# All moving operands of the large matmuls at one place relative to the weights, and new rates for VectorE

## The chip, the cores and the metric

The kernel runs on one core of a Trainium2 chip. The core has TensorE (PE in the profile; its weight loads are listed apart as PEld), VectorE (DVE), ScalarE (ACT), GpSimd (POOL) and SyncE (SP, which here issues the DMAs). The metric is the device time in microseconds of one execution, median over runs.

## The reference

One inference step of a two-layer backbone for two groups of requests that share all weights: 128 context tokens (`x_prompt`) and 128 latent tokens (`x_sample`), model width 2048. Cut to its shape:

```python
for l in range(2):
    mod = silu(cond) @ w_ada[l] + b_ada[l]            # 2048 -> 6 x 2048
    sh1, sc1, gt1, sh2, sc2, gt2 = split(mod, 6)
    h = rmsnorm(x, g_norm_mix[l]) * (1 + sc1) + sh1
    m = mixer_ab(h, ...) if l % 2 == 0 else mixer_c(h, ...)
    x = x + gt1 * m
    h = rmsnorm(x, g_norm_ffn[l]) * (1 + sc2) + sh2
    u = conv3(h @ w_up[l]) + b_conv                   # 2048 -> 2 x 5632, width-3 conv over tokens
    x = x + gt2 * ((silu(u_gate) * u_val) @ w_down[l])
return rmsnorm(x, g_final), new context tensors
```

`mixer_ab` is latent attention and grouped-query attention side by side (one input projection `w_in_ab`, two up-projections `w_q_up` and `w_kv_up`, one output projection `w_out_ab`); `mixer_c` is differential attention (`w_in_c`, `w_out_c`). Everything is float32. The latent tokens attend to 128 cached context keys as well, and the context group also returns its keys and values.

## The kernel before, in words

Features lie on the 128 partitions and tokens along the row, so one tile of activations is 128 features by 256 tokens (both groups side by side, `NT = 256`). All large products go through one function, `gemm` (lines 234 to 244): for each block of 128 x 128 weights it issues three matmuls of 256 columns, `wh*xh`, `wh*xl` and `wl*xh`, where the weights and the activations are split into a rounded part (`wh`, `xh`) and a rest (`wl`, `xl`), so that the product is nearly that of float32. Each matmul has a weight load of its own.

The weights stream in. `Weights.chunk` (line 209) lets SP load 1 MB into a `raw` buffer (three of them), ScalarE rounds it to `wh` (line 195), VectorE subtracts to get `wl` (line 196); `wh` and `wl` have four buffers of eight blocks each, every block 512 bytes of a partition's row.

The moving operands are rows of `ROW = 2 * NT + 8` floats, that is 520 floats or 2080 bytes: 256 of `xh`, 256 of `xl`, eight unused. Such rows make up `hx` (16 rows, the modulated input of a stage, and also the output of the first mixer's heads), `o_all` (16 rows, output of the odd layer's heads) and the `g` tiles (22 tiles, the gated FFN activations). Two smaller operands have other shapes: `ql` (rows of 2048 bytes, for `w_q_up`) and `kv_in` (rows of 384 floats, for `w_kv_up`).

The stages, in order: `w_in_ab` in four parts (its input chunks are ready one quarter after another); heads; `w_out_ab`; FFN of layer 0 as two halves, each `up` (44 groups of 16 blocks) and `down` (16 groups of 22 blocks); `w_in_c` with the odd layer's heads; `w_out_c`; FFN of layer 1; the last norm. Between stages `modulated` (line 445) makes the next `hx`: the sum of squares is finished on PE (`stat_rstd`, lines 175 and 176), `rv` (166), a power on POOL (168), `diag` (182), `spread` on PE (190), then for each of 16 chunks a product `nt` (430), scale and shift (436 on VectorE, 439 on ScalarE), rounding (440) and the rest (442, VectorE or POOL in turn). `fill` (line 401) puts row units there for PE.

The products `silu(cond) @ w_ada`, nearly 200 loads of 1 MB, are spread over the whole time in two ways. `row_step` (line 339) loads a tile `araw` (two buffers) and sums it on PE with four matmuls a tile (`sum_rows`, line 334). `feature_step` (line 311) does one half of a tile on VectorE: a product of 2048 elements with a row sum (line 319, its output tile is called `junk`); two steps share one load into `araw`, eight steps make one unit of `FEATS`, and the steps are kept in program order.

`pump` (line 384) is called after each `gemm` and adds a rate to what is due; a `feature_step` runs whenever a whole one is due. In the FFN the rates are `FRATE` (line 51): one for each `up` group (none for the first six groups of a layer) and one for each `down` group (none for the last four of half 1). At the end of `ffn` a loop runs what is left up to the stage's limit (`FLIMIT`, 13 units, or 104 steps, for layer 0; 15 units in all for layer 1). A scheduler then orders each engine's instructions by its own estimate of time.

Of the kernel before, what the change touches and what calls it, by code (L numbers as in the profile page):

```python
# [17 lines left out]
P = 128  # L18
# [1 line left out]
KD = D // P  # L20
T = 128
NT = 2 * T
ROW = 2 * NT + 8
NL = 2
GRID_W = 64
EPS = 1e-6
# [21 lines left out]
    _n += _w  # L48
NCONST = _n
RATE = {"in": 0.4, "in3": 0.25, "heads": 0.85, "out0": 1.2, "c": 0.65, "outc": 0.65}  # L50
FRATE = {"up": 0.75, "down": 1.55}
PEW = {"heads": 1.0, "out0": 1.0, "c": 0.5}
QUIET = [4, 3, 3]
LATE = 3
# [21 lines left out]
def step_kernel(ctx: ExitStack, tc: tile.TileContext, A: dict):  # L76
# [4 lines left out]
    wpool = ctx.enter_context(tc.tile_pool(name="wpool", bufs=3))  # L81
# [8 lines left out]
    def banks(name):  # L90
        return tc.tile_pool(name=name, bufs=1, space=PSUM)
# [3 lines left out]
    def nm(s):  # L95
        uid[0] += 1
        return f"{s}_{uid[0]}"

    def T_(pl, shape, tag, dt=F32, bufs=None):
        kw = {} if bufs is None else {"bufs": bufs}  # L100
        return pl.tile(shape, dt, tag=tag, name=nm(tag), **kw)


    cst = T_(keep, [P, NCONST], "cst")
# [21 lines left out]
    def load_cw(l):  # L126
        ada["cw"] = T_(keep, [P, 4, 2 * NFF], "convw")
        sp.dma_start(out=ada["cw"], in_=A["wconv"][:, l])
# [65 lines left out]
    def split(out_hi, out_lo, src):  # L194
        act.copy(out_hi, src)  # L195
        dve.tensor_tensor(out=out_lo, in0=src, in1=out_hi.bitcast(F32), op=ALU.subtract)  # L196
# [37 lines left out]
    def gemm(blocks, xh, xl, n=NT, first=0):  # L234

        ps = T_(pacc, [P, 512], "acc")
        last = len(blocks) - 1
        for i in range(last + 1):
            k = (i + first) % (last + 1)
            wh, wl = blocks[k]  # L240
            pe.matmul(ps[:, :n], wh, xh(k), start=(i == 0), stop=False)  # L241
            pe.matmul(ps[:, :n], wh, xl(k), start=False, stop=False)  # L242
            pe.matmul(ps[:, :n], wl, xh(k), start=False, stop=(i == last))  # L243
        return ps[:, :n]
# [60 lines left out]
    def load_row():  # L305
        feat["row"] = T_(feat["home"], [P, 2, D], "condb")
        sp.dma_start(out=feat["row"], in_=A["condb"])
        for r in range(2):
            act.activation(feat["row"][:, r], feat["row"][:, r], AF.Silu)
# [74 lines left out]
    def pump(rows, feats=0.0, until=None):  # L384

        until = until or RLIMIT[stage[0]]
        step()
        ada["due"] += rows
        while ada["due"] >= 0.25:
            if ada["i"] >= until and not later:  # L390
                ada["due"] = 0.0
                break
            dve_or_none = ada["i"] >= until or ada["i"] in SUMMED
            ada["due"] -= 0.25 if dve_or_none else 0.25 * ada["pew"]
            row_step(until)
        feat["due"] += feats
        while feat["due"] >= 1.0 and feat["i"] < FLIMIT[stage[0]]:
            feat["due"] -= 1.0
            feature_step()
# [13 lines left out]
    def ensure(l, j, qs=range(4)):  # L413
        for u in [(l, j, q) for q in qs]:
            while u in ROWS and ada["i"] <= ROWS.index(u):
                row_step()
            while u in FEATS and u not in done:
                feature_step()
            while u not in done:
                later.pop(0)()  # L420


    def norm_scale(st):
        return spread(diagonal(stat_rstd(st, D), (0, 1)))

    def modulate(hx, rb, l, which, chunks):

        for c in chunks:
            h = T_(tmp, [P, NT], "nt", bufs=4)
            dve.tensor_tensor(out=h, in0=x[:, c], in1=rb, op=ALU.mult)  # L430
            for g in range(2):
                s = slice(g * T, (g + 1) * T)
                a_ = scl[:, l, which, c, g:g + 1]
                b_ = mod[:, l, 3 * which, c, g:g + 1]
                if g == 0:
                    dve.tensor_scalar(out=h[:, s], in0=h[:, s], scalar1=a_, scalar2=b_,  # L436
                                      op0=ALU.mult, op1=ALU.add)
                else:
                    act.activation(h[:, s], h[:, s], AF.Identity, scale=a_, bias=b_)
            act.copy(hx[:, c, :NT], h)  # L440
            eng = pool if c % 2 else dve
            eng.tensor_tensor(out=hx[:, c, NT:2 * NT], in0=h, in1=hx[:, c, :NT].bitcast(F32),
                              op=ALU.subtract)

    def modulated(st, l, which, units):
        ensure(l, 3 * which + 1)
        ensure(l, 3 * which)
        hx = T_(keep, [P, KD, ROW], "hx", F32R)
        modulate(hx, norm_scale(st), l, which, range(KD))
# [75 lines left out]
    def mixer_ab(hx, rb0, st):  # L525
        l = 0
        with tc.tile_pool(name="ab", bufs=1) as ab:
            with tc.tile_pool(name="abp", bufs=1) as pj:
                kv_in = T_(ab, [P, 4, 2, 3 * T], "kv_in", F32R)
                ckc = T_(pj, [P, 4, T], "ckc")  # L530
                kr = T_(ab, [P, 3 * T], "kr")
# [125 lines left out]
            with tc.tile_pool(name="abh", bufs=1) as hp:  # L657
                ada["pew"] = PEW["heads"]

                o = T_(keep, [P, KD, ROW], "hx", F32R)  # L660
                load_cw(0)
# [79 lines left out]
    def mixer_c(cp, hx, st):  # L741
# [12 lines left out]
        W = Weights(A["w_in_c"], KD, 1)  # L754
        xh, xl = (lambda k: hx[:, k, :NT]), (lambda k: hx[:, k, NT:2 * NT])
        outs = []
        o_all = T_(cp, [P, KD, ROW], "oall", F32R)

        def project(h):
# [98 lines left out]
    def ffn(hx, l, st):  # L858
        xh, xl = (lambda k: hx[:, k, :NT]), (lambda k: hx[:, k, NT:2 * NT])
        W = Weights(A["w_up"][l], KD, 1)  # L860
        WD = Weights(A["w_down"][l], KQ, TB)
        cw = ada["cw"]
        with tc.tile_pool(name=f"ffn{l}", bufs=1) as fp, banks(f"pffn{l}") as pf:
            feat["home"], feat["pool"] = fp, pf

            def conv(ps, m):
                y = T_(fp, [P, NT], "cv", bufs=3)
                act.activation(y, ps, AF.Identity, scale=cw[:, 1, m:m + 1], bias=cw[:, 3, m:m + 1])  # L868
                y3 = y.rearrange("p (g t) -> p g t", g=2)
                p3 = ps.rearrange("p (g t) -> p g t", g=2)  # L870
                dve.scalar_tensor_tensor(out=y3[:, :, 1:], in0=p3[:, :, :T - 1],  # L871
                                         scalar=cw[:, 0, m:m + 1], in1=y3[:, :, 1:],
                                         op0=ALU.mult, op1=ALU.add)
                dve.scalar_tensor_tensor(out=y3[:, :, :T - 1], in0=p3[:, :, 1:],  # L874
                                         scalar=cw[:, 2, m:m + 1], in1=y3[:, :, :T - 1],
                                         op0=ALU.mult, op1=ALU.add)
                return y

            def up(q):
                gs = []  # L880
                for i in range(q * KQ, (q + 1) * KQ):
                    rate = 0 if i < LATE else FRATE["up"]
                    fine[0] = False
                    gate = conv(gemm(W.chunk(), xh, xl), i)
                    pump(0, rate)
                    if i == 0:
                        load_row()
                    val = conv(gemm(W.chunk(), xh, xl), NFF + i)
                    pump(0, rate)
                    act.activation(gate, gate, AF.Silu)  # L890
                    dve.tensor_tensor(out=val, in0=gate, in1=val, op=ALU.mult)
                    g = T_(fp, [P, ROW], "g", F32R, bufs=KQ)
                    split(g[:, :NT], g[:, NT:2 * NT], val)
                    gs.append(g)
                return gs

            def down(gs, q):
                for c in range(KD):
                    quiet = q == NQ - 1 and c >= KD - QUIET[0]
                    fine[0] = quiet  # L900
                    ps = gemm(WD.chunk(), lambda k: gs[k][:, :NT], lambda k: gs[k][:, NT:2 * NT])
                    residual(ps, l, 1, c, st if q == NQ - 1 else None)
                    pump(0, 0 if quiet else FRATE["down"])

            for q in range(NQ):
                gs = up(q)
                if q == 0:
                    ensure(l, 5)
                down(gs, q)
            while feat["i"] < FLIMIT[stage[0]]:  # L910
                feature_step()


    with banks("pab") as ppool["ada"]:
# [6 lines left out]
        for c in range(KD):  # L921
            stat_add(st, x[:, c], KD)
        hx = T_(keep, [P, KD, ROW], "hx", F32R)
        rb0 = norm_scale(st)
# [7 lines left out]
    with tc.tile_pool(name="cc", bufs=1) as cp, banks("pc") as ppool["ada"]:  # L932
        ada["pool"] = cp
        ppool["att"] = ppool["ada"]
        hx = modulated(st, 1, 0, 2)
        load_cw(1)
        st = stat_init()
        ada["pew"] = PEW["c"]
        mixer_c(cp, hx, st)
        hx = modulated(st, 1, 1, 2)  # L940
# [136 lines left out]
```

## Time and profile before

| | |
|---|---|
| median of three runs | 2475.45 us (2472.75 to 2478.08) |
| the profiled execution | 2474.37 us, span 2472.3 us |
| TensorE busy | 2408.7 us, 97% of the span |
| VectorE busy | 1766.5 us, 71% |
| ScalarE busy | 1156.3 us, 47% |
| bytes moved by DMA | 612.92 MB, mean 248 GB/s |

How to read it: times are microseconds from the first instruction unless marked ns. A group of instructions is a line with its engine, operation, `out<-in` by the kernel's names, shapes and count, then busy time and mean ns of one, then the engine's idle time before it and what ended most of that. Matmuls are pipelined, so the length of one says little; the distance between starts is what it costs. A row of busy time by stretch has the stretch, its length, and for each engine the busy time and the count of instructions that touch it, then PEclk (the TensorE clock that was granted, 1.00 is full), the DMA engines' busy share and GB/s; its last row sums all stretches. In a row in order of time stand the start, the length, the engine (a q behind it marks its queue, which issues DMAs), the line, the operation, and in square brackets the idle time before it and what ended it.

### The profile page before, as it was taken

The page shows a single profiled execution, that of the slowest core. Times are in us where ns is not written, and L with a number is a line of the kernel's source. Part 1 is how long each engine was busy: PE and PEld are TensorE (multiplying, and loading weights), DVE is VectorE, ACT ScalarE, POOL GpSimd, SP SyncE. Part 2 cuts the span into 40 slices and gives each one's busy share as a digit, 9 for nine tenths or more (in the row PEclk, how much of TensorE's full clock was granted, in tenths as well). Part 3 has the DMA queues.
Part 4 walks back from the last instruction along what each step waited for, and adds up shares of the span by engine and source line. Part 5 has one row for each costly group of instructions (what it writes and reads, how often), then busy time and mean ns, then how long its engine had stood idle before and what let it go on. Part 6 is the DMA issues. An engine that isn't in the chain of part 4 may idle for free.

```text
span 2472.3 us, 47301 instructions
## 1 busy us (share of the span) xinstructions
PE 2408.7 (97%) x19664; PEld 2268.5 (92%) x19664; DVE 1766.5 (71%) x2699; ACT 1156.3 (47%) x1815; POOL 170.4 (7%) x211
## 2 busy tenths in 40 slices
PE   6999999999999999999999999999999999999997
PEld 4778768799999999999979999897999999999997
DVE  2457534578898999999869897766897655666654
ACT  4335544454553345554455454446545433555442
POOL 2002101100000000001210101021000000000011
PEclk9999999999999999999999999999999999999999
DMA  9886668867677776677776777757665555555553
GB/s 383 311 322 244 231 259 305 320 252 251 255 265 272 292 269 252 250 267 273 279 281 241 275 255 269 279 205 283 242 243 188 188 188 188 186 184 184 183 188 117
DMA packets 92549, 612.92 MB, mean 248 GB/s; under 512 B 9968, under 2 KB 17840, under 8 KB 20400
## 3 DMA queue, kind: packets, MB, share of 16 engines
q1 hardware_dynamic: 92336, 609.91, 67.5%
q8 instruction: 154, 2.52, 0.4%
q14 instruction: 59, 0.48, 0.1%
HBM read 605.12 MB, written 4.75 MB: 247 GB/s over the span
## 4 chain that ended last, share of the span: by engine, by line
PE 94%; DMA 2%; issue 1%; DVE 1%; ACT 1%; POOL 0%; POOLq 0%; SPq 0%; DVEq 0%; ACTq 0%
PE acc L241 29%; PE acc L242 29%; PE acc L243 29%; PE ada L334 4%; DMA araw<-w_ada 1%; PE att L505 1%; DMA ckc<-cache_ckv 1%; PE ada L282 1%; DMA raw<-w_in_ab 0%; PE att L795 0%; DMA raw<-w_ada 0%; PE att L495 0%; DVE x L946 0%; PE ada L269 0%; DVE nt L436 0%
## 5 line engine op out<-in xcount | busy, mean ns | idle before, releaser
L195 ACT CAST wh<-raw 128x1024 fp32r<-128x1024 f32 (+1 forms) x788 | 792.0, 1010 | 1097.2 <-PE acc L242 937.7
L196 DVE TENSOR_TENSOR wl<-raw,wh 128x1024 fp32r<-128x1024 f32 (+1 forms) x788 | 923.8, 1181 | 457.1 <-ACT wh L195 454.3
L241 PE MATMUL acc<-hx,wh 128*128 128x256 f32 x4208 | 1192.7, 285 | 10.9 <-ACT hx L440 10.1
L242 PE MATMUL acc<-hx,wh 128*128 128x256 f32 x4208 | 1186.1, 282 | 0.0
L243 PE MATMUL acc<-hx,wl 128*128 128x256 f32 x4208 | 1185.3, 282 | 0.0
L241 PEld LDWEIGHTS acc<-hx,wh 128*128 128x128 f32 x4208 | 794.0, 189 | 47.8 <-ACT hx L440 19.7
L242 PEld LDWEIGHTS acc<-hx,wh 128*128 128x128 f32 x4208 | 797.2, 190 | 20.5 <-issue 18.7
L243 PEld LDWEIGHTS acc<-hx,wl 128*128 128x128 f32 x4208 | 796.6, 189 | 12.2 <-issue 12.1
L243 PE MATMUL acc<-g,wl 128*128 128x256 f32 x1408 | 394.4, 281 | 0.0
L241 PE MATMUL acc<-g,wh 128*128 128x256 f32 x1408 | 393.9, 280 | 0.0
L242 PE MATMUL acc<-g,wh 128*128 128x256 f32 x1408 | 393.6, 280 | 0.0
L319 DVE CUSTOM_DVE_ANT_0 junk<-araw,condb 128x2048 f32<-128x2048 f32 x120 | 275.4, 2295 | 0.0
L242 PEld LDWEIGHTS acc<-g,wh 128*128 128x128 f32 x1408 | 265.3, 188 | 0.0
L243 PEld LDWEIGHTS acc<-g,wl 128*128 128x128 f32 x1408 | 265.1, 188 | 0.0
L241 PEld LDWEIGHTS acc<-g,wh 128*128 128x128 f32 x1408 | 264.7, 188 | 0.0
L161 POOL TENSOR_TENSOR sqacc<-sqacc,sq 128x256 f32<-128x256 f32 x76 | 91.3, 1201 | 1595.9 <-issue 1274.1
L334 PE MATMUL ada<-araw,condw 128*32 128x512 f32 x864 | 123.3, 646 | 18.8 <-DMA araw<-w_ada 17.9
L363 DVE SCALAR_TENSOR_TENSOR aacc<-araw,condw,aacc 128x512 f32<-128x512 f32 x150 | 107.8, 749 | 0.3
L456 DVE SCALAR_TENSOR_TENSOR x<-acc,mod,x 128x128 f32<-128x128 f32 x192 | 58.3, 345 | 59.6 <-PE acc L243 59.5
L868 ACT ACTIVATE cv<-acc,convw 128x256 f32<-128x256 f32 x176 | 98.4, 559 | 0.0
L874 DVE SCALAR_TENSOR_TENSOR cv<-acc,convw,cv 128x254 f32<-128x254 f32 x176 | 84.3, 479 | 3.7
L871 DVE SCALAR_TENSOR_TENSOR cv<-acc,convw,cv 128x254 f32<-128x254 f32 x176 | 83.8, 476 | 0.0
(195 smaller groups left out, 1625.5 us busy)
## 6 DMA issues: line engine op xcount, KB each, us to landing
araw<-w_ada SPq DMA_DIRECT2D x188, 1024.0 KB, 6.1
raw<-w_up SPq DMA_DIRECT2D x176, 1024.0 KB, 4.8
raw<-w_down SPq DMA_DIRECT2D x88, 1024.0 KB, 4.8
raw<-w_in_c SPq DMA_DIRECT2D x48, 1024.0 KB, 5.2
raw<-w_in_ab SPq DMA_DIRECT2D x20, 1024.0 KB, 7.2
raw<-w_out_ab SPq DMA_DIRECT2D x16, 1024.0 KB, 6.8
raw<-w_out_c SPq DMA_DIRECT2D x16, 1024.0 KB, 4.8
raw<-w_q_up SPq DMA_DIRECT2D x6, 768.0 KB, 4.5
```

The costliest lines, as they stand in the source:

```text
L161: pool.tensor_tensor(out=st["acc"], in0=st["acc"], in1=sq, op=ALU.add)
L195: act.copy(out_hi, src)
L196: dve.tensor_tensor(out=out_lo, in0=src, in1=out_hi.bitcast(F32), op=ALU.subtract)
L241: pe.matmul(ps[:, :n], wh, xh(k), start=(i == 0), stop=False)
L242: pe.matmul(ps[:, :n], wh, xl(k), start=False, stop=False)
L243: pe.matmul(ps[:, :n], wl, xh(k), start=False, stop=(i == last))
L319: tc.keep_in_program_order(dve.tensor_tensor_reduce(out=T_(feat["pool"], [P, D], "junk"), in1=feat["row"][:, c], in0=feat["raw"].rearrange ...
L334: i = pe.matmul(ada["ps"][32 * g:32 * g + 32, :], condw[:, 4 * t + g, :], raw[:, g], start=(t == 0), stop=(t == 3), skip_group_check=True)
L363: i = dve.scalar_tensor_tensor(out=acc[:, c], in0=raw[:, g], scalar=condw[:, k, c:c + 1], in1=acc[:, c], op0=ALU.mult, op1=ALU.add)
L868: act.activation(y, ps, AF.Identity, scale=cw[:, 1, m:m + 1], bias=cw[:, 3, m:m + 1])
L871: dve.scalar_tensor_tensor(out=y3[:, :, 1:], in0=p3[:, :, :T - 1], scalar=cw[:, 0, m:m + 1], in1=y3[:, :, 1:], op0=ALU.mult, op1=ALU.add)
L874: dve.scalar_tensor_tensor(out=y3[:, :, :T - 1], in0=p3[:, :, 1:], scalar=cw[:, 2, m:m + 1], in1=y3[:, :, :T - 1], op0=ALU.mult, op1=ALU.add)
```

## The change

`ROW` loses its eight unused floats, so each row is 2048 bytes, a multiple of 512. Since a weight block is 512 bytes, a moving operand's address relative to the weights, modulo 512, is then the same for every block of a tensor. Unused tiles (`pad`) are put ahead of `kv_in`, `o_all` and the FFN's tiles, and one of 192 bytes into the weights' pool, so that this place is 448 bytes for all of `hx`, `ql`, `kv_in`, `o_all` and `g`. Before, `ql` and `kv_in` were at place 0 and the others moved on by 32 bytes from row to row through all sixteen places. The two rates in `FRATE` are lowered.

```diff
-ROW = 2 * NT + 8
+ROW = 2 * NT
+SHIFT = 448
...
-FRATE = {"up": 0.75, "down": 1.55}
+FRATE = {"up": 0.735, "down": 1.435}
...
+    T_(wpool, [P, 48], "pad", bufs=1)
...
             with tc.tile_pool(name="abp", bufs=1) as pj:
+                T_(ab, [P, SHIFT // 4], "pad")
                 kv_in = T_(ab, [P, 4, 2, 3 * T], "kv_in", F32R)
...
+        T_(cp, [P, SHIFT // 4 - 24], "pad")
         o_all = T_(cp, [P, KD, ROW], "oall", F32R)
...
         with tc.tile_pool(name=f"ffn{l}", bufs=1) as fp, banks(f"pffn{l}") as pf:
             feat["home"], feat["pool"] = fp, pf
+            T_(fp, [P, SHIFT // 4], "pad")
```

## The prediction

> **What bounds the kernel now.** I read the page first (busy time, clock, chain of waits), then busy time by stage, then the matmuls by the place of their moving operand, and last the gap before the odd layer in order of time.
>
> ```profile
> span 2472.3 us, 47301 instructions
> PE 2408.7 (97%) x19664; PEld 2268.5 (92%) x19664; DVE 1766.5 (71%) x2699; ACT 1156.3 (47%) x1815; POOL 170.4 (7%) x211
> ...
> PE 94%; DMA 2%; issue 1%; DVE 1%; ACT 1%; POOL 0%; POOLq 0%; SPq 0%; DVEq 0%; ACTq 0%
> ...
> L241 PE MATMUL acc<-hx,wh 128*128 128x256 f32 x4208 | 1192.7, 285 | 10.9 <-ACT hx L440 10.1
> ...
> L241 PE MATMUL acc<-g,wh 128*128 128x256 f32 x1408 | 393.9, 280 | 0.0
> ...
> L319 DVE CUSTOM_DVE_ANT_0 junk<-araw,condb 128x2048 f32<-128x2048 f32 x120 | 275.4, 2295 | 0.0
> ```
>
> TensorE is the chain (94%). The three lines of `gemm` (241 to 243) have 3 x 4208 matmuls from `hx` and `o`, and 3 x 1408 from `g`; a mean of 285 ns is the length of one in the pipeline, not its price. The price is the time from one start to the next, which whole stages without a gap give:
>
> ```profile
> core 0: us, PE busy (x) PEld busy (x) DVE busy (x) ACT busy (x) POOL busy (x), PEclk, DMA share, GB/s
> 745.80:870.05 124.25, 124.25 (x1059) 124.25 (x1058) 114.48 (x133) 47.28 (x48) 0.00 (x0) 1.00 0.76 284
> 870.05:1119.90 249.85, 249.85 (x2114) 249.85 (x2113) 227.86 (x291) 125.52 (x174) 0.00 (x0) 1.00 0.71 259
> 2083.30:2333.20 249.90, 249.90 (x2115) 249.90 (x2114) 162.08 (x218) 125.74 (x174) 0.00 (x0) 1.00 0.53 186
> ```
>
> The first is a down half (16 x 22 x 3 = 1056 matmuls; the count has two or three more that reach in): 124.25 / 1056 = 117.7 ns. The others are up halves (44 x 16 x 3 = 2112): 118.3 ns. Both at full clock and with PE never idle. VectorE's busy share there, 91% and 92% in layer 0 but 65% in layer 1, does not show in the price. So the bound is what one matmul with its weight load costs.
>
> **Does the place matter?** In the kernel before, a row of `hx` or `g` is 2080 bytes = 4 x 512 + 32, and a weight block 512 bytes, so the moving operand's place relative to the weights moves by 32 bytes from block to block: upwards in the stages that read `hx`, `o` and `o_all` (in `up` it begins at 128), downwards in `down`, where the `g` buffers are met in falling order. `ql` has rows of 2048 bytes and stands at place 0 throughout. I cut the trace at the start of each block's first matmul and summed stretches of equal place modulo 256 (places 256 apart measured alike).
>
> ```profile
> sum 30.57, PE 30.57; mean PE 0.35
> sum 31.38, PE 31.38; mean PE 0.36
> sum 31.63, PE 31.63; mean PE 0.36
> sum 10.21, PE 10.21; mean PE 0.12
> sum 10.56, PE 10.56; mean PE 0.12
> sum 45.11, PE 45.11; mean PE 0.35
> sum 68.05, PE 68.05; mean PE 0.35
> sum 67.22, PE 67.22; mean PE 0.35
> sum 15.04, PE 15.04; mean PE 0.12
> sum 22.62, PE 22.62; mean PE 0.12
> ...
> 223.41:225.44 2.03, 2.03 (x19) 1.00 0.84 315
> ...
> sum 21.27, PE 21.27; mean PE 2.36
> ```
>
> Rows 1 to 3: the 88 blocks (264 matmuls) of the up half at 2083.30 at places 192 (which is 448 too), 0 and 32: 115.8, 118.9 and 119.8 ns a matmul; 192 is the lowest of the eight places, 32 the highest. Rows 4 and 5: of the same blocks the second matmul alone (same place before and after it), at 192 and at 0: 116.0 and 120.0. Rows 6 to 8: the four down halves, 128 blocks at 192, 192 at 0, 192 at 64: 117.5, 118.1 and 116.7, so going down 192 isn't the lowest; rows 9 and 10, the second matmuls at 192 and 0: 117.5 and 117.8. The last two are `ql`, nine unbroken stretches with 178 steps at the fixed place 0, the first with 17: 21.27 / 178 = 119.5 ns.
>
> So the place is worth up to 4 ns in 118, and the neighbours' place too, since 192 costs 116.0 on the way up and 117.5 on the way down. No row shows a fixed place 448; `ql` shows a fixed place 0, and there the fixed price (119.5) lies between the second matmul going down (117.8) and going up (120.0), three quarters of the way to the upward one. The same share at 192, from 117.5 towards 116.0, gives 116.3 to 116.4; I take 116.3. Added to the mean of both directions at 192 (116.6), the surplus that `ql` has over that mean at 0 (119.5 against 118.5) would give 117.6. Ends: 117.5 (that, and the downward row), and 115.2 (as far below row 1 as `ql` lies above row 2, 0.65 ns).
>
> Against this stands a rule of the Trainium skill. Its page "TensorE: Matmul & The Clock Gate", section "Step-by-step: what each phase is for", says that TensorE has two independent SBUF read ports and that loading the next weights takes no read bandwidth from the running matmul. By that rule the places would be worth nothing; the rows above disagree (115.8 against 119.8 ns), so the sum goes by the rows, and the rule is the second rival.
>
> **The sum on TensorE**, in counts from the code:
> - Upward stages at 118.33: `up` 4 x 2112, `w_in_c` 2304, `w_out_c` 768, `w_out_ab` 768, `w_in_ab` 1104, in all 13,392. x 2.03 = 27.2 us.
> - `down` at 117.65: 4 x 1056 = 4224 x 1.35 = 5.7 us.
> - `ql`: 216 x 3.2 = 0.7 us. `kv_in` (192 matmuls of 384 columns, place 0 before): no row at another place; 0 to 0.6, I take 0.3.
> - Less 1.1, half of the gain of `w_in_ab`: in that stage PE also waits for `hx`, as this row of the waits from 40 to 223 us has it, and a faster matmul waits longer.
>
> ```profile
> PE acc L241 <- ACT hx L440: 5.6, 3, 2.9
> ```
>
> Gain 32.8 us. At 117.5 it would be 11.1 + 0.6 + 0.4 = 12; at 115.2, 41.9 + 10.3 + 0.9 = 53. Transposes, attention products and the four-column `ada` sums keep their number; some move by a place and I cost them at nothing, being some 8% of PE's instructions and not lined up by the change. The pads cost only SBUF.
>
> **The rates.** `feature_step` is 104 steps before the end of layer 0's FFN. The old rates give 82 x 0.75 + 28 x 1.55 = 104.9 there, so all are done inside the gemms. The new ones give 82 x 0.735 + 28 x 1.435 = 100.45: four steps are left to the loop at the end of `ffn`, and the built program has them on VectorE between the last residual and the first `hx` of the next stage: one after the residual, one after `rv`, one after `diag`, one after the first four `nt`. The stretch before:
>
> ```profile
> L319 DVE DVE_READ_ACCUMULATOR2_ANT mod<- x120: 132/141/145, 546.7 to 1868.1; 128x1 f32 x120
> ...
> 1244.26 0.61 DVE L456 SCALAR_TENSOR_TENSOR x<-acc,mod,x 128x128 f32<-128x128 f32 x2 [0.58 <-PE acc L243]
> ...
> 1245.27 1.23 DVE L196 TENSOR_TENSOR wl<-raw,wh 128x1024 fp32r<-128x1024 f32 x1 [0.34 <-ACT wh L195]
> 1246.99 0.16 DVE L166 TENSOR_SCALAR rv<-misc 128x2 f32<-128x2 f32 x1 [0.49 <-PE misc L176]
> 1247.96 0.48 DVE L182 TENSOR_SCALAR diag<-cst,rr 128x128 f32<-128x128 f32 x2 [0.81 <-POOL rr L168]
> 1249.82 1.41 DVE L430 TENSOR_TENSOR nt<-x,misc 128x256 f32<-128x256 f32 x4 [1.38 <-PE misc L190]
> 1251.15 1.11 DVE L436 TENSOR_SCALAR nt<-nt,scl,mod 128x128 f32<-128x128 f32 x4
> ```
>
> A step is 2.29 + 0.14 = 2.43 us, four 9.7. VectorE idles in this stretch 0.34 + 0.49 + 0.81 + 1.38 = 3.0 us, so the first `hx` comes 6.7 later: `rv` by 1.6, `diag` by 3.2, `nt` by 4.2, the scaling by 6.7. Taking the four steps out of `down` gives nothing back, as PE has no gap there. TensorE's own side:
>
> ```profile
> 1244.27 1.92 PE L334 MATMUL ada<-araw,condw 128*32 128x512 f32 x16
> 1248.59 1.19 PE L190 MATMUL misc<-diag,cst 128*128 128x256 f32 x2 [1.64 <-DVE diag L182]
> 1251.52 1.94 PE L334 MATMUL ada<-araw,condw 128*32 128x512 f32 x8 [1.74 <-DMA araw<-w_ada]
> ...
> 1219.23 0.33 SPq L354 DMA_DIRECT2D araw<-w_ada  x1
> 1245.67 0.47 SPq L354 DMA_DIRECT2D araw<-w_ada  x1
> ...
> araw<-w_ada SPq DMA_DIRECT2D x188, 1024.0 KB, 6.1
> ...
> 1248.40:1255.20 6.80, 4.87 (x18) 2.49 (x18) 5.39 (x16) 4.18 (x12) 1.60 (x2) 0.50 0.97 371
> ```
>
> The 16 filler matmuls at 1244.27, whose weights were fetched at 1219, ran in a time when PE could do nothing else. The four steps' two loads now hold both `araw` buffers, SP's queue has these filler loads after the `w_in_c` ones, and the program has no filler ahead of `spread`: 1.9 us of PE work goes to where `hx` is being made. Its first group waits for the second step (1251.1) and 6.1 us of load, 1257.2, then runs up to 1.9: PE's first large matmul comes about 6 us later by this way too, alongside the 6.7, not on top. I take 7 (the 6.7 and a little of the fillers). Ends: 4.2, if the fourth step hides behind ScalarE's half of the scaling, and 13: 9.7 + 1.9 + 1.7, if the half clock that the last row shows after this wait (6.8 us at 0.50) lasts half as long again, 3.4 us.
>
> VectorE keeps its cover: an up half of layer 0 loses 44 x 0.015 x 2.43 = 1.6 us of steps and gets 226.3 us in 2112 x 116.3 = 245.6, 92%; a down half 110.0 in 122.8, 90%. Without the lower rates both would be 93%. In layer 1 only 16 steps are due and the shares are lower.
>
> **Sum.** The profiled execution took 2474.37 (span 2472.3 and 2.1 around it), 1.1 below the median of the three runs. 2474.4 - 32.8 + 7 = 2448.6, say 2449, 1.0% less.
>
> **Rivals.**
> 1. The fixed place locks the two streams badly. For it: 192 costs 117.5 among falling places, and the one fixed place on record is dearer than its rows by block (119.5 against 118.9 and 118.1). And going down 64 is cheaper than 192 (116.7). Against it: the mean of both directions is lowest at 192, 116.6, and next at 64, 118.0; a fixed place, which mixes no neighbours in, should make such a difference larger, as it did at 0. At `ql`'s price: 13,392 x 1.2 + 4224 x 1.85 = 24 us lost, and 7: 2505. It decides from 117.8 ns on, where the mean before (118.17) less 7 us over 17,616 matmuls stands.
> 2. The place as such is worth nothing (the price follows something that went with it, such as the block's position in its gemm): no gain, 7 lost, 2481. For it nothing but that place and position go together in `up`; against it, places 256 apart are 8 positions apart and measured alike.
> 3. VectorE becomes the bound in layer 0's FFN, at 92%: there the gain (4224 x 2.03 + 2112 x 1.35 = 11.4) is lost, 2460. Against it: 91% and 92% cost PE nothing before.
>
> **Chances.** Forecast (a price of 115.2 to 117.5) 0.74; rival 3, 0.07; rival 1 with all prices over 117.5, 0.14, of which 0.05 within 0.2%; rival 2, 0.05. So faster by over 0.2% 0.81, within it 0.05, slower 0.14; 0.2% is about what a measurement of this kernel can tell from no change. Likeliest case alone: 2474 - 53 + 4 = 2426 to 2474 - 12 + 7 = 2469. The range goes to 2474, with 13 for the gap.
>
> **What would show it.** Right: up halves near 245.6 us and down halves near 122.8, both alike per matmul; no digit of PE below 9 in layer 0's FFN; four `junk` steps near 1230 us, and the next stage's first matmul some 15 to 16 us after the last `down` one, 9.3 before. Wrong: halves of 250 us or more (rivals 1 and 2), or waits of `acc` for `wl` or `cv` in layer 0's FFN alone (rival 3). What I trust least is the step from moving places to one fixed place.

## The result and the profile after

The changed kernel takes 2405.8 us (median of four runs, 2405.0 to 2409.0) against 2474.1 before: the ratio is 0.972, with a 95% interval of 0.971 to 0.974. It was forecast faster, and it is faster by 2.7 times what was forecast; the time lies below the range.

The page of the changed kernel (its lines stand four to seven further down in the code: 245 to 247 are 241 to 243 before, 323 is 319):

```profile
span 2404.2 us, 47304 instructions
PE 2329.8 (97%) x19664; PEld 2190.5 (91%) x19664; DVE 1764.9 (73%) x2699; ACT 1161.7 (48%) x1815; POOL 176.3 (7%) x211
...
PE 92%; DMA 4%; DVE 2%; issue 1%; ACT 1%; POOL 0%; POOLq 0%; SPq 0%; DVEq 0%; ACTq 0%
...
L245 PE MATMUL acc<-hx,wh 128*128 128x256 f32 x4208 | 1170.8, 280 | 12.0 <-ACT hx L444 11.4
...
L245 PE MATMUL acc<-g,wh 128*128 128x256 f32 x1408 | 387.9, 276 | 0.0
...
L323 DVE CUSTOM_DVE_ANT_0 junk<-araw,condb 128x2048 f32<-128x2048 f32 x120 | 274.6, 2288 | 0.0
```

TensorE is still the chain, with the same instructions. Only the length of a matmul has moved, and, as before, the distance between starts says more. Busy time by stretch (columns: stretch, its length, then PE, PEld, DVE, ACT and POOL busy with counts, PEclk, DMA share, GB/s): a down half and an up half of layer 0, the gap before the odd layer (from the first statistics matmul to the first matmul on `hx`), an up half of layer 1:

```profile
726.43:846.11 119.68, 119.68 (x1058) 119.68 (x1057) 111.23 (x131) 47.10 (x46) 0.00 (x0) 1.00 0.78 288
846.11:1085.47 239.36, 239.36 (x2114) 239.36 (x2113) 224.33 (x287) 126.72 (x174) 0.00 (x0) 1.00 0.73 266
...
1205.15:1220.37 15.22, 4.16 (x20) 1.64 (x19) 14.49 (x26) 4.33 (x10) 3.52 (x2) 0.68 0.50 181
...
2030.64:2270.00 239.36, 239.36 (x2114) 239.36 (x2113) 162.06 (x218) 126.76 (x174) 0.00 (x0) 1.00 0.55 194
```

and the same gap in the kernel before:

```profile
1244.06:1253.39 9.33, 5.95 (x36) 2.06 (x35) 6.08 (x18) 4.39 (x11) 1.48 (x3) 0.73 0.85 303
```

Up halves: 239.36 / 2112 = 113.3 ns, from 118.3. Down halves: 119.68 / 1056 = 113.3 ns, from 117.7. So the four up halves give about 42 us, the four down halves 18, the gap takes 5.9 back, and the other stages give the remaining 14 of the 68.1 by which the span is shorter.

### The profile page after: what moved, and what is told of

Same layout as the page of the kernel before. It is cut to its first block, busy times and chain, and to the rows that moved or that the text cites. A ratio compares the mean times of both kernels' runs of the same rounds, so it can differ in the third digit from the quotient of the medians.

```text
span 2404.2 us, 47304 instructions
## 1 busy us (share of the span) xinstructions
PE 2329.8 (97%) x19664; PEld 2190.5 (91%) x19664; DVE 1764.9 (73%) x2699; ACT 1161.7 (48%) x1815; POOL 176.3 (7%) x211
## 4 chain that ended last, share of the span: by engine, by line
PE 92%; DMA 4%; DVE 2%; issue 1%; ACT 1%; POOL 0%; POOLq 0%; SPq 0%; DVEq 0%; ACTq 0%
PE acc L245 28%; PE acc L246 28%; PE acc L247 28%; PE ada L338 4%; DMA araw<-w_ada 2%; PE att L509 1%; DMA ckc<-cache_ckv 1%; DMA raw<-w_in_ab 0%; PE ada L286 0%; PE att L801 0%; PE att L499 0%; DMA raw<-w_ada 0%; DMA condb<-condb 0%; DVE nt L440 0%; DVE x L953 0%
## 5 line engine op out<-in xcount | busy, mean ns | idle before, releaser
L245 PE MATMUL acc<-hx,wh 128*128 128x256 f32 x4208 | 1170.8, 280 | 12.0 <-ACT hx L444 11.4
L246 PE MATMUL acc<-hx,wh 128*128 128x256 f32 x4208 | 1170.2, 279 | 0.4 <-DVE hx L446 0.4
L247 PE MATMUL acc<-hx,wl 128*128 128x256 f32 x4208 | 1169.0, 278 | 0.0
L246 PE MATMUL acc<-g,wh 128*128 128x256 f32 x1408 | 388.3, 276 | 0.0
L247 PE MATMUL acc<-g,wl 128*128 128x256 f32 x1408 | 388.1, 276 | 0.0
L245 PE MATMUL acc<-g,wh 128*128 128x256 f32 x1408 | 387.9, 276 | 0.0
L338 PE MATMUL ada<-araw,condw 128*32 128x512 f32 x864 | 121.3, 635 | 22.7 <-DMA araw<-w_ada 17.2
```

Of the source, the lines that this page charges most:

```text
L338: i = pe.matmul(ada["ps"][32 * g:32 * g + 32, :], condw[:, 4 * t + g, :], raw[:, g], start=(t == 0), stop=(t == 3), skip_group_check=True)
```

## The experiments

Two theories were formed on the result. Theory A: at a fixed place the stream of matmuls settles into a pattern with a price of its own, which depends on the place modulo 256; where the place moves, rows sorted by place do not show these prices. Theory B, its rival: what counts is only that the place stands still. A second question was what the rates do.

**The rates alone.**

```diff
 # the kernel before
-FRATE = {"up": 0.75, "down": 1.55}
+FRATE = {"up": 0.735, "down": 1.435}
```

> The kernel before with the two new rates alone (rows still 2080 bytes). Both theories: the price of a matmul stays (118.3 ns in the up halves, 117.6 in the down halves), four VectorE steps come into the gap before the odd layer, which grows from 9.3 us to about 15, and the time by 5 to 7 us, to about 2480. If the rates carry part of the gain, it is under 2470.

Measured: 2481.7 us against 2474.0, ratio 1.003 (1.002 to 1.004). An up half, and the gap:

```profile
868.51:1118.42 249.91, 249.91 (x2114) 249.91 (x2113) 225.30 (x289) 125.55 (x174) 0.00 (x0) 1.00 0.70 255
...
1242.61:1257.83 15.22, 4.17 (x20) 1.65 (x19) 14.49 (x26) 4.34 (x10) 3.52 (x2) 0.63 0.48 175
```

The price stays at 118.3 ns, and the gap is 15.22 us, as in the changed kernel. The rates carry none of the gain.

**The places alone.**

```diff
 # the changed kernel
-FRATE = {"up": 0.735, "down": 1.435}
+FRATE = {"up": 0.75, "down": 1.55}
```

> The changed kernel with the old rates 0.75 and 1.55: all 104 VectorE steps are done inside layer 0's FFN. If VectorE keeps up: the price stays 113.3 ns, the gap before the odd layer goes back from 15.1 us to 9 to 10, time about 2400. If VectorE becomes the bound at the faster pace (its busy share in layer 0's down halves would be 96 to 97%): the halves of layer 0 are longer than the 239.4 and 119.7 us of layer 1's, and the 5 to 6 us are lost there: 2406 or more.

Measured: 2397.6 us, ratio to before 0.970 (0.968 to 0.972). A down half and an up half of layer 0, and the gap:

```profile
726.21:845.89 119.68, 119.68 (x1058) 119.68 (x1057) 113.94 (x134) 47.40 (x47) 0.00 (x0) 1.00 0.79 297
845.89:1085.25 239.36, 239.36 (x2114) 239.36 (x2113) 226.65 (x289) 126.45 (x174) 0.00 (x0) 1.00 0.74 271
...
1205.44:1214.17 8.73, 5.42 (x36) 1.85 (x35) 6.00 (x18) 4.31 (x11) 1.41 (x3) 0.83 0.90 319
```

VectorE is busy for 95% of both halves and PE does not wait there: the lengths are those of the changed kernel to the hundredth. The gap is 8.73 us. In layer 0's FFN PE waits for VectorE only in the second down half, once:

```profile
1085.25:1205.44 120.19, 119.97 (x1058) 119.77 (x1057) 110.15 (x132) 53.39 (x71) 21.12 (x14) 1.00 0.76 282
...
PE acc L247 <- DVE wl L200: 0.2, 1, 0.2
```

That half is 0.5 us longer than in the changed kernel (119.68), against 6.5 us that the gap gives back. The lower rates were not needed.

**Other fixed places, two kernels, one run each.** The pads give every operand a place of its own. The pad in `wpool` moves the weights and leaves `hx` where it was, so between these kernels and the changed one `hx` moves only relative to the weights:

```diff
 # the changed kernel; first kernel: hx 0, ql and kv_in 224, g0 32, g1 64, o_all 192
 # second kernel: hx 224, ql and kv_in 0, g0 96, g1 128, o_all 160
-    T_(wpool, [P, 48], "pad", bufs=1)
+    T_(wpool, [P, 32], "pad", bufs=1)          # second: 104
...
-                T_(ab, [P, SHIFT // 4], "pad")
+                T_(ab, [P, PLACE["ab"] // 4], "pad")   # second: left out
...
-        T_(cp, [P, SHIFT // 4 - 24], "pad")
+        T_(cp, [P, (PLACE["oall"] - 96) % 512 // 4], "pad")
...
-            T_(fp, [P, SHIFT // 4], "pad")
+            T_(fp, [P, PLACE[f"g{l}"] // 4], "pad")
```

> The changed kernel with fixed places of its own for each operand: hx 0, ql and kv_in 224, g of layer 0 at 32, g of layer 1 at 64, o_all at 192. Theory A (the two read streams lock, and the price follows the place modulo 256): hx at 0 costs about 119.5 ns, as ql did at 0 in the kernel before, so the up halves take 252 us in place of 239.4 and the kernel about 2480; o_all at 192 shows the same two prices as at 448, 113.3 and 117.8; the g places differ from each other. Theory B (what counts is only that the place no longer moves): every stage at 113.3 ns, the up halves 239.4 us, time about 2406.

> As the run before, with hx at 224, ql and kv_in at 0, g of layer 0 at 96, g of layer 1 at 128, o_all at 160. Theory A: ql at 0 costs 119.5 ns again, the other places each a price of its own between 113 and 120, constant for long stretches, with jumps only where something else came between the matmuls. Theory B: 113.3 ns everywhere, about 2406 us.

Measured: 2499.8 and 2498.1 us, beside 2474.0 before. First kernel: down half of layer 0 (`g` at 32), up half (`hx` at 0), down half of layer 1 (`g` at 64), and of PE alone the longest unbroken stretch of `w_out_c` (`o_all` at 192), from its first start to its last:

```profile
751.98:876.36 124.38, 124.38 (x1058) 124.38 (x1057) 110.79 (x130) 46.99 (x46) 0.00 (x0) 1.00 0.75 275
876.36:1129.80 253.43, 253.43 (x2114) 253.43 (x2113) 226.38 (x289) 125.49 (x174) 0.00 (x0) 1.00 0.69 252
...
1980.81:2105.18 124.38, 124.38 (x1058) 124.38 (x1057) 63.77 (x78) 46.87 (x46) 0.00 (x0) 1.00 0.52 186
...
1646.59:1706.67 60.08, 60.08 (x532) 1.00 0.57 201
```

Second kernel, the same rows (`g` at 96, `hx` at 224, `g` at 128), and two unbroken stretches of `w_out_c` (`o_all` at 160), of 88 and of 530 matmuls:

```profile
751.63:878.34 126.72, 126.72 (x1058) 126.72 (x1057) 111.28 (x131) 46.86 (x46) 0.00 (x0) 1.00 0.74 272
878.34:1128.26 249.92, 249.92 (x2114) 249.92 (x2113) 225.24 (x289) 125.64 (x174) 0.00 (x0) 1.00 0.70 254
...
1978.48:2105.20 126.72, 126.72 (x1058) 126.72 (x1057) 63.89 (x78) 47.09 (x46) 0.00 (x0) 1.00 0.52 183
...
1606.55:1616.87 10.33, 10.33 (x90) 1.00 0.66 229
1644.87:1707.77 62.90, 62.90 (x532) 1.00 0.54 192
```

By length over 2112, 1056 or, in the last rows, the count less two (530 and 88):

| place modulo 256 | 0 | 32 | 64 | 96 | 128 | 160 | 192 | 224 |
|---|---|---|---|---|---|---|---|---|
| ns a matmul, fixed | 120.0 | 117.8 | 117.8 | 120.0 | 120.0 | 117.4 and 118.7 | 113.4 | 118.3 |

B falls: standing still is worth nothing by itself, and at 0, 96 and 128 it is dearer than moving. A holds: 192, which is 448 modulo 256, costs as much as 448 did and stands 4 ns or more below the others. The mean of the eight is 118.2 (with 118.7 for 160), and moving places cost 118.3 upwards and 117.7 downwards: a moving operand pays about the mean. Two misses: the first kernel was expected at about 2480 us and took 20 more, and the second price that 448 has (117.8 ns, see the end) was expected at 192 too, where that long stretch shows only the low one. In the table operand and place go together; where two operands held one place, they agree or nearly so: 448 costs `hx` and `g` the same, and `ql` at 0, in the second kernel, took 119.4 ns by the starts (119.5 expected) beside the 120.0 of `hx`.

**A place that changes by turns.** `hx` is made of two half tiles with a gap between them, and row k is looked up in one or the other:

```diff
+    class Rows:
+        def __init__(self):
+            self.a = T_(keep, [P, KD // 2, ROW], "hx", F32R)
+            T_(keep, [P, 64], "hxpad")                      # 56 floats for 160
+            self.b = T_(keep, [P, KD // 2, ROW], "hxb", F32R)
+        def __getitem__(self, at):
+            p, k, cols = at
+            tile, row = (self.a, self.b)[k % 2], k // 2     # halves: [k // 8], k % 8
+            return tile[p, row, cols]
...
-        hx = T_(keep, [P, KD, ROW], "hx", F32R)
+        hx = Rows()
```

The pad in `wpool` is set so that the first half tile stays at 448.

> The changed kernel, but the rows of hx stand by turns at 448 and at 192 (two half tiles with 256 unused bytes between them); all else at 448. If the price follows the place modulo 256: up halves stay at 113.3 ns a matmul (239.4 us), time about 2406. If it follows the place modulo 512, or if any change of place from block to block costs: 115 ns or more, up halves of 243 us or more, time over 2415.

Measured: 2406.3 us, and an up half of the same length as the changed kernel's:

```profile
848.35:1087.71 239.36, 239.36 (x2114) 239.36 (x2113) 224.39 (x287) 126.76 (x174) 0.00 (x0) 1.00 0.73 266
```

So for this pair the price goes by the place modulo 256: sixteen changes a group between 448 and 192 cost nothing.

> As the run before, but by turns at 448 and 160, two places that cost 113.3 and (o_all in the fourth run) 118.5 ns when fixed. Theory A1 (each block costs what its own place costs): the mean, 115.9 ns, up halves 244.8 us. Theory A2 (the cheap pattern needs a run at one place to be reached; a change every three matmuls prevents it): 117 ns or more, up halves of 247 us or more, as with the moving places of the kernel before.

> As the run before, but with rows 0 to 7 at 448 and rows 8 to 15 at 160: two changes of place in a group of sixteen blocks in place of sixteen. A1: 115.9 ns as in the run before. A2: near 115.9 ns too, but clearly under the run before, since each place holds for 24 matmuls.

Measured: 2444.2 us by turns, 2435.8 in halves. By turns: an up half, then 176 blocks (528 matmuls) at 448 and 176 at 160 of another up half, cut at each block's first matmul as in the prediction:

```profile
859.82:1106.21 246.39, 246.39 (x2114) 246.39 (x2113) 224.61 (x287) 125.55 (x174) 0.00 (x0) 1.00 0.71 259
...
sum 61.08, PE 61.08; mean PE 0.35
sum 62.12, PE 62.12; mean PE 0.35
```

In halves, the same three:

```profile
858.37:1103.27 244.90, 244.90 (x2114) 244.90 (x2113) 224.56 (x287) 125.77 (x174) 0.00 (x0) 1.00 0.71 260
...
sum 60.52, PE 60.52; mean PE 0.34
sum 61.91, PE 61.91; mean PE 0.35
```

By turns 116.7 ns, between A1 (115.9) and A2 (117 or more); in halves 116.0, as both had it. What matters for the prediction is in the other rows. By turns, the blocks at 448 show 61.08 / 528 = 115.7 ns, though 448 costs 113.3 when fixed. In halves they show 60.52 / 528 = 114.6, and there it can be seen where the surplus sits. Of the same stretch, from the second group on, the first two blocks after each change to 448, and the six blocks behind them:

```profile
sum 14.96, PE 14.96; mean PE 0.71
...
sum 42.84, PE 42.84; mean PE 2.04
```

That is 14.96 / 126 = 118.7 ns and 42.84 / 378 = 113.3. After a change of place the cheap price is there only from the third block on, as A2 had it, and by turns it is never reached. The blocks at 160 show 117.7 by turns and 117.3 in halves; since 160 has 117.4 and 118.7 when fixed, they say little. In a stream whose place changes, the row of a place is not its fixed price: it also holds what the change costs.

**Sixteen bytes to either side.** `hx` in one tile with eight floats more, its rows read from the fifth on; everything else stays at 448:

```diff
-        hx = T_(keep, [P, KD, ROW], "hx", F32R)
+        hx = Rows()     # one tile [P, KD * ROW + 8], row k from k * ROW + 4 on
...
-    T_(wpool, [P, 48], "pad", bufs=1)
+    T_(wpool, [P, 40], "pad", bufs=1)          # 464; left at 48 it is 432
```

> The changed kernel with hx at 464, between 448 (113.3 ns, with stretches of 117.8) and 224 modulo 256 (118.3 ns); all else at 448. Theory A gives a price of its own, between 113 and 118 ns; if the good pattern is a broad one with 448 near its edge, the stretches of 117.8 ns in the stage of w_in_c go away and the up halves stay at 239.4 us; if 448 is its middle or its other edge, up halves cost 247 us or more.

> The changed kernel with hx at 432, 16 bytes on the other side of 448; all else at 448. 464 cost 119.2 ns. If the good place is one notch wide, 432 costs 117 ns or more (up halves 247 us or more, time over 2440); if it reaches down to 432, up halves stay near 239.4 us, perhaps without the dearer stretches in the stage of w_in_c.

Measured: 2467.0 us at 464, 2474.3 at 432, each with an up half here:

```profile
864.87:1116.55 251.68, 251.68 (x2114) 251.68 (x2113) 225.83 (x289) 125.57 (x174) 0.00 (x0) 1.00 0.70 254
```

```profile
869.34:1121.22 251.88, 251.88 (x2114) 251.88 (x2113) 225.85 (x289) 125.60 (x174) 0.00 (x0) 1.00 0.69 253
```

119.2 and 119.3 ns, against 113.3 between them. The cheap place reaches less than 16 bytes to each side, so being at the edge of something broader is ruled out as the reason for the dearer stretches that 448 has too. Theory A's figure was missed: it put 464 between 113 and 118, and 464 costs more than either neighbour, 448 and 224 (118.3).

**Both again, side by side:** the changed kernel, and the one with the places alone, both as they were.

> The changed kernel once more, beside the next run on the same chip. About 2406 us. If the two prices at place 448 (113.3 and 117.8 ns) are chosen by chance at each start, w_out_c, which ran at 117.0 ns in the first profile, may run at 113.3 in this one (2.8 us less); if the program fixes it, it is at 117 again.

> The fixed places with the old rates once more. By the gap before the odd layer (15.1 us against 8.6) it is 5 to 7 us faster than the run before, about 2399; if its earlier lead of 8 us came from the cheap price in w_out_c alone, the two are within 3 us.

Measured: 2405.2 us, ratio to before 0.972 (0.971 to 0.973), and 2397.8 us, 0.969 (0.968 to 0.970). The gap in the second is

```profile
1205.27:1214.77 9.50, 5.42 (x36) 1.85 (x35) 6.77 (x19) 4.72 (x11) 2.18 (x3) 0.81 0.90 315
```

against 15.22 in the first: 5.7 of the 7.4 us. The places with the old rates are the version that beats both kernels. As to `w_out_c`, from its first matmul to its last: the changed kernel, the places alone, and the places alone again.

```profile
1547.63:1650.43 102.80, 97.60 (x798) 95.29 (x797) 72.72 (x116) 42.73 (x71) 21.93 (x19) 0.97 0.59 212
```

```profile
1539.84:1640.83 100.99, 96.16 (x798) 93.74 (x797) 72.63 (x116) 42.61 (x71) 21.36 (x19) 0.95 0.61 215
```

```profile
1539.77:1643.01 103.23, 98.40 (x798) 95.97 (x797) 72.61 (x116) 42.55 (x71) 21.44 (x19) 0.95 0.60 213
```

The last two are one program in two executions, 2.2 us apart; the changed kernel's second profile stays dear (104.85, with a longer wait in it). Its second run by itself fits either case of its expectation; the other pair shows that one program can have either price, and the lead of the places alone does not come from there.

## Why the prediction was right or wrong

**The price of a fixed place was wrong**, and it is the step the prediction trusted least. It read 115.8 (upwards) and 117.5 (downwards) at 192 and reasoned: "The same share at 192, from 117.5 towards 116.0, gives 116.3 to 116.4; I take 116.3", with 115.2 as the lowest price it allowed. The price is 113.3. The runs by turns and in halves show why: a row cut out of a stream of changing places is no price of its place. By turns the very same place read 115.7, nearly what it read in the kernel before, while its fixed price was 113.3; in halves the 113.3 came back from the third block after each change on. In the kernel before the place changed at every block. The rule that the prediction carried over from `ql`, whose fixed price at 0 lies three quarters of the way from the downward to the upward row, had no ground: fixed prices spread from 113.3 to 120.0 where the upward rows by place spread from 115.8 to 119.8, so a low row should have been taken further down and not up to the middle. The prediction named this ("should make such a difference larger") and didn't use it.

What each row of a moving stream is made of stays open. It is not simply a mean of its neighbours' fixed prices: 192 read 115.8 upwards and 117.5 downwards with the same two neighbours in the other order, and 64 downwards read 116.7, below the fixed prices of 32, 64 and 96.

The sum with the right price: 13,392 x 5.0 + 4224 x 4.3 = 85 us in place of 32.9, of which the profile shows 42 in `up` (17.1 forecast) and 18 in `down` (5.7). The other stages would give 25 by this; they gave 14. By the starts, some 1,800 matmuls of these stages took 116 to 120 ns, 448's dearer price for the most part, which is 8 of the missing 11 us; the rest was not taken apart.

**Whether the place matters: right.** With the same instructions on TensorE, `hx` at 0 costs 120.0 ns and at 448 113.3. So rival 2 fell. The Trainium skill ("TensorE: Matmul & The Clock Gate", "Step-by-step: what each phase is for") says that loading the next weights takes no read bandwidth from the running matmul. What the prediction drew from it, that the places would then be worth nothing, is not so here; whether reads collide no run shows. Rival 1, that a fixed place could be dear, holds at the other places by its own point of decision (117.8 ns), at 0, 96 and 128 by far, at 32 and 64 only just, and at 160 in its long stretch; 448 is the exception.

**The rates: right.** Four steps were left over and came where the prediction put them. VectorE in the gap of the changed kernel, in order of time:

```profile
1205.36 0.61 DVE L460 SCALAR_TENSOR_TENSOR x<-acc,mod,x 128x128 f32<-128x128 f32 x2 [0.48 <-PE acc L247]
1205.88 2.29 DVE L323 CUSTOM_DVE_ANT_0 junk<-araw,condb 128x2048 f32<-128x2048 f32 x1
...
1209.22 0.15 DVE L170 TENSOR_SCALAR rv<-misc 128x2 f32<-128x2 f32 x1
1209.29 2.29 DVE L323 CUSTOM_DVE_ANT_0 junk<-araw,condb 128x2048 f32<-128x2048 f32 x1
...
1212.17 0.48 DVE L186 TENSOR_SCALAR diag<-cst,rr 128x128 f32<-128x128 f32 x2 [0.53 <-POOL rr L172]
1212.56 2.29 DVE L323 CUSTOM_DVE_ANT_0 junk<-araw,condb 128x2048 f32<-128x2048 f32 x1
...
1214.78 1.41 DVE L434 TENSOR_TENSOR nt<-x,misc 128x256 f32<-128x256 f32 x4
1216.10 2.29 DVE L323 CUSTOM_DVE_ANT_0 junk<-araw,condb 128x2048 f32<-128x2048 f32 x1
...
1218.31 1.11 DVE L440 TENSOR_SCALAR nt<-nt,scl,mod 128x128 f32<-128x128 f32 x4
```

From the residual to `nt` 9.4 us (5.6 before, so 3.9 later; forecast 4.2), to the scaling 12.95 (6.9 before, 6.1 later; forecast 6.7). And PE:

```profile
1212.80 1.19 PE L194 MATMUL misc<-diag,cst 128*128 128x256 f32 x2 [4.98 <-DVE diag L186]
1218.51 1.94 PE L338 MATMUL ada<-araw,condw 128*32 128x512 f32 x8 [4.52 <-DVE mod L323]
1220.37 0.80 PE L245 MATMUL acc<-hx,wh 128*128 128x256 f32 x2
```

The fillers (L338) start 13.4 us into the gap (forecast 13.1), by the profile released by the fourth step where the forecast had them wait for their load, and the first large matmul follows them. The gap is 15.2 us where 15 to 16 was forecast, 5.9 more than before (7 forecast); alone, the rates cost 7.7 us by the device time, with an interval of about 4.5 to 10.

**VectorE's cover: right, and there was more of it.** Rival 3 fell: with VectorE at 94% in the changed kernel PE did not wait for it, and at 95% with the old rates it waited once, in a half that became 0.5 us longer. The prediction had worked out 92% and 90% for the slower pace it expected, and 93% without the lower rates, which it costed at 7 us; the places alone confirm that they were not needed.

## What to carry to other kernels

A price that depends on a state which changes from one instruction to the next should not be read off rows sorted by that state: here such a row also held what the change costs and the true spread was wider than the rows showed; one run with the state held still settles it. Where TensorE is the bound and each matmul brings a weight load, try the placement of the moving operand against the weights: here the best place of eight was 4% below a moving operand, and none of the other seven gained even 1%. And before a background rate is lowered to make room, count what is left over and where the program puts it: 3.5 steps too few put four on the critical gap.

## What the runs showed of the hardware that was not expected

The price follows the place modulo 256 bytes (tried for 448 and 192), takes a few values (113.3 to 120.0 ns at steps of 32 bytes) and is 119.2 only 16 bytes from the best. At the best place there are two prices, as at 160. PE in two stretches of 10 us of the changed kernel, both without other work, one in the stage of `w_in_c` and one in `w_out_c`:

```profile
1310.00:1320.00 10.00, 10.00 (x90) 1.00 0.75 286
1620.00:1630.00 10.00, 10.00 (x87) 1.00 0.61 211
```

Less the two that reach in, 88 and 85 matmuls: 113.6 and 117.6 ns as counted, 113.3 and 117.8 by the starts. A price holds until something else comes between the matmuls, and may differ after it; the FFN halves always ran at the lower one after their first groups, `w_in_c` partly and the long last stretch of `w_out_c` in six of the nine profiles with `o_all` at 448 at the higher. What chooses between them wasn't found, nor tried beyond the repeats. That the moving operand's reads and the weight load's reads collide in the memory is a reading that fits all this, but no run shows the collision itself. The Trainium skill ("TensorE: Matmul & The Clock Gate", "Back-to-back issue gap") gives N / 2.4 + 2.5 ns as the gap of an isolated matmul; for 256 columns that is, by estimate, 109.2 ns. The cheapest pattern here is 4 ns over that, and no run reached it.
